# Token sums on VectorE alone and a last down-projection segment of four chunks

## The chip, the cores and the metric

The kernel runs on one core of a Trainium2 chip. The core has TensorE (PE, matrix products), VectorE (DVE), ScalarE (ACT), GpSimd (POOL), SyncE (SP, which here issues the transfers) and DMA engines between DRAM and SBUF. Each engine works through its own list of instructions in order; semaphores join the lists. The metric is the time of one launch in device microseconds. Matmuls write to PSUM banks of 128 x 512 f32, and a bank must be read out before a later group of matmuls may use it again.

## The reference

One layer of an encoder for 256 + 1024 = 1280 tokens with width 1024, all in float32. The change touches the second feed-forward layer and what follows:

```
def swiglu(h, w_gu, w_down):
    gate, up = jnp.split(h @ w_gu, 2, axis=-1)
    return (jax.nn.silu(gate) * up) @ w_down

x = x + 0.5 * rms_norm(swiglu(rms_norm(x, ffn2_pre_g), ffn2_w_gu, ffn2_w_down), ffn2_post_g)
x = rms_norm(x, final_g)
```

The hidden width is 2816, that is 22 chunks of 128. Each f32 product is made of three matmuls of rounded parts (high by high, high by low, low by high), so every operand is split into a high part (a cast on ScalarE) and a low part (a subtraction on VectorE).

## The kernel before

**Order.** The program is written as Python loops, and a scheduler that simulates a timeline sets the order of each engine's list from them and from the dependences. An edit in one place can therefore move instructions of all engines near it.

**Up-projection (`ffn_gu`).** The tokens form three tiles: 0 and 1 with 512 tokens, 2 with 256. The transposed activations of tile t lie in `hT[t]` as parts h and l. Chunks 0 and 1 are "plain": for each tile and each of gate and up (s = 0, 1), `gu` runs 8 x 3 matmuls into a bank `psgu`; then ScalarE takes the silu of the gate, VectorE multiplies it with up (`ac`, L513), and the product is stored to the DRAM tensor `ad`. The tiles run in the order 2, 0, 1 for chunk 0 and 1, 0, 2 for chunk 1. After each half, `post` converts weights and makes pieces of side work.

The other 20 chunks go by `pair`, which computes gate and up of a chunk with seven products where eight would be plain (a scheme of Strassen's kind on 2 x 2 blocks of weights and tokens). For it `token_sums` prepares, once, sums and differences of the token blocks of tiles 0 and 1: T1 to T4, each split in h and l, made in two halves (i = 0, 1) by the steps t1, t3, t2, t4 and by `then`, which overwrites `hT[1]` with T1. Of these sums VectorE does some (`v`), GpSimd four per half (`g`: L459, L471, L472, L478). A VectorE or GpSimd sum is 128 x 1024. Before, the steps begin in chunk 1, two in each `post`.

**Down-projection (`ffn_down`).** The 22 chunks are added up in segments of 1, 3, 3, 3, 3, 3, 3, 3 chunks. In a segment all ten blocks of 128 tokens (b = 0 to 9) run one after another; a block's product of a segment's chunks goes into a pair of banks `psd` (two pairs are in use), and is then copied (segment 0: L660 on VectorE for odd blocks, L662 on ScalarE for even ones) or added (L664, VectorE) to the block's row of y, which lies in the memory of `hT` (tiles named yh0h, yh0l, yh2h). A chunk of weights is loaded as 512 KB `raw` (L612) and split into `wd` (L634 on ScalarE, L635 on VectorE); activations are read back from `ad` as `ar` (L617) and split into `ahl`. `load_to` and `conv_to` walk a list of such units; units ahead of segment 0 are made during the last pair, which `pre` does.

**The end.** In the last segment each finished block goes through `chain`: s1 loads the residual row `xr` (L246) and takes sums of squares (ScalarE L206, then GpSimd's two one-column operations L207 and L208), s2 scales (L212, VectorE) and adds the residual (L254, on GpSimd for blocks 0, 1, 2, 4 and 6, on VectorE for the others), s3 takes the second sum of squares, s4 scales again and sends the row out (L271).

Of the kernel before, what the change touches and what calls it, by code (L numbers as in the profile page):

```python
# [10 lines left out]
F32 = mybir.dt.float32  # L11
# [137 lines left out]
class Trunk:  # L149
# [53 lines left out]
    def rstd(self, src, junk, mul):  # L203
        nc = self.nc
        st = self.stp.tile([P, 2], F32, name="st", tag="st", bufs=8)
        nc.scalar.activation(junk, src, AF.Square, scale=D ** -0.5 / mul, accum_out=st[:, 0:1])  # L206
        nc.gpsimd.tensor_scalar(st[:, 0:1], st[:, 0:1], 1e-6 / (mul * mul), None, op0=OP.add)  # L207
        nc.gpsimd.tensor_tensor(st[:, 1:2], st[:, 0:1], self.mhalf, op=OP.pow)  # L208
        return st[:, 1:2]
# [24 lines left out]
    def chain(self, src, xrows, mul, gpost, gnext, spill=None, out=None, inplace=True):  # L234
# [14 lines left out]
        def s2(b):  # L249
            x, tmp, r = V[b]  # L250
            y = src(b) if inplace else tmp
            self.scaled(y, src(b), r, gpost)
            if inplace:
                (nc.gpsimd if out is None or b in (0, 1, 2, 4, 6) else nc.vector).tensor_tensor(y, y, x, op=OP.add)  # L254
            else:
                nc.gpsimd.tensor_tensor(x, x, y, op=OP.add)
                y = x
            V[b] = y
# [181 lines left out]
    def token_sums(self, tpool):  # L440
        nc = self.nc
        v, g = nc.vector.tensor_tensor, nc.gpsimd.tensor_tensor
        T = {k: [tpool.tile([P, 4, 512], F32R, name=f"T{k}{s}") for s in "hl"] for k in (2, 3, 4)}
# [3 lines left out]
        def split(k, r, src):  # L447
            hi, lo = (z[:, r] for z in T[k])
            nc.scalar.activation(hi, src, AF.Copy)
            v(lo, src, hi.bitcast(F32), op=OP.subtract)  # L450

        for i in range(2):
            r, r2 = slice(2 * i, 2 * i + 2), slice(2 * i + 4, 2 * i + 6)
            b11, b21, b12, b22 = ([z[:, q].bitcast(F32) for z in self.hT[t]] for t in (0, 1) for q in (r, r2))
            Z = {}

            def t1(Z=Z, b11=b11, b12=b12):
                Z[1], Z[0] = self.tmp("x", (P, 2, 512)), self.tmp("g", (P, 2, 512))
                g(Z[0], b12[1], b11[1], op=OP.subtract)  # L459
                v(Z[1], b12[0], b11[0], op=OP.subtract)  # L460
                v(Z[1], Z[1], Z[0], op=OP.add)

            def t2(Z=Z, b22=b22, r=r):
                Z[2] = self.tmp("tmp", (P, 2, 512))
                v(Z[2], b22[0], Z[1], op=OP.subtract)
                v(Z[2], Z[2], b22[1], op=OP.add)
                split(2, r, Z[2])

            def t3(Z=Z, b22=b22, b12=b12, r=r):
                z, o = self.tmp("g", (P, 2, 512)), Z.pop(0)  # L470
                g(o, b22[1], b12[1], op=OP.subtract)  # L471
                g(z, b22[0], b12[0], op=OP.subtract)  # L472
                v(z, z, o, op=OP.add)
                split(3, r, z)

            def t4(Z=Z, b21=b21, r=r):
                z = Z[2]
                g(z, b21[0], z, op=OP.subtract)  # L478
                v(z, z, b21[1], op=OP.add)
                split(4, r, z)  # L480

            first += [t1, t3, t2, t4]
            then.append(lambda Z=Z, r=r: split(1, r, Z[1]))
        return T, first, then

    def ffn_gu(self, pool, tpool, S, W, ad, orders, prep=None):
# [76 lines left out]

        T, first, then = {}, [], []
        for f, order in enumerate(orders):
            for z, t in enumerate(order):
                last = f == len(orders) - 1

                def post(s):
                    n = 2 * f + 3 + (z > 0)  # L570
                    if n <= len(S.units):
                        S.conv_to(n)
                    elif z or s:
                        W.to(1 if first else 3)
                    if last and first:
                        for _ in range(2):
                            first.pop(0)()
                    elif last and then and 1 in order[:z + 1 if s else z]:
                        then.pop(0)()
                gu(f, t, post)  # L580
                if f == 0 and z == 2:
                    t_, a_, b_ = self.token_sums(tpool)
                    T |= t_
                    first += a_
                    then += b_
        for z in first + then:
# [7 lines left out]
    def ffn_down(self, ad, w_down, segs):  # L594
# [26 lines left out]
        def conv_to(n, ahead=3):  # L621
            while st["c"] < min(n, len(units)):
# [13 lines left out]
                st["c"] += 1  # L636
                load_to(min(st["c"] + ahead, npre if st["c"] <= npre and ahead < 3 else 1 << 30))

        pre = [lambda i=i: conv_to(i + 1, 1) for i in range(npre)]

# [538 lines left out]
def run(self):  # L1179
# [124 lines left out]

    def place(c, what):
        if what == "x":
            return pools["p"].tile([P, D], F32, name="xr", tag="wd", bufs=6)
        p = pools.get("p")
        if what == "raw":
            return (p or self.wp).tile([P, D], F32, name="raw", tag="rw" if p else "raw", bufs=2)  # L1310
        if p is None:
# [4 lines left out]
    self.place = place  # L1316
    pre, go = self.ffn_down(ad, a["ffn2_w_down"], (1, 3, 3, 3, 3, 3, 3, 3))
    self.ffn_gu(fa, ft, S2, Pairs(self, a["ffn2_w_gu"], 2, pre), ad, ((2, 0, 1), (1, 0, 2)))
# [48 lines left out]
```

## Time and profile before

The time is the median of 3 runs, 2462.53 us (2461.67 to 2463.34). The profiled execution took 2464.15 us, of which 2462.4 are the span from the first to the last instruction that is shown.

| stage of the profiled execution | us from the span's start |
|---|---|
| plain chunks 0 and 1 of the second layer, token sums beside them | about 1559 to 1622.4 |
| 20 pairs | 1622.4 to about 2120 |
| down-projection, segment 0, overlapping the last pair's end | about 2120 to 2143.1 |
| segments 1 to 7, ten blocks of 4.2 us each | 2143.1 to 2438.2 |
| from the last matmul to the end | 2438.2 to 2462.4 |

How to read it: "busy" is the time in which an engine executes; a wait names the engine, line and tile that the waiting engine was released by. In rows in order of time the first number is the start, the second the duration, and brackets give the idle time before and its releaser. `out<-in` are tiles. Matmuls overlap, so the distance between starts tells their pace, not the duration. The clock is that granted to TensorE, as a share of full speed.

### The profile page before, as it was taken

What the parts mean: (1) busy time and instruction counts of PE and PEld (TensorE: products, weight loads), DVE (VectorE), ACT (ScalarE), POOL (GpSimd) and SP (SyncE); (2) the same over time, 40 slices, a digit from 0 to 9 for tenths busy, and PEclk for the clock granted to TensorE, in tenths of its full rate; (3) what the DMA queues carried; (4) which work ended last, traced back from release to release, by engine and by line L of the source; (5) the groups of instructions that cost most, each with busy time, mean ns of one, the idle gap of its engine ahead of it and who ended that gap; (6) DMA issues with size and microseconds to landing.
All of it is one profiled execution on the core that took longest, in us unless ns stands there. A gap on an engine that the chain in (4) does not pass through costs nothing.

```text
span 2462.4 us, 30177 instructions
## 1 busy us (share of the span) xinstructions
PE 2368.3 (96%) x12028; PEld 2011.2 (82%) x12028; DVE 1270.2 (52%) x1684; ACT 740.0 (30%) x1387; POOL 532.4 (22%) x487
## 2 busy tenths in 40 slices
PE   7999999999999999999988889999999999999995
PEld 7888888888888877888877778888888888788884
DVE  5344444444444448898355553754434434545447
ACT  5211111111111124664365642232222222312113
POOL 2000000000000025796112323532323223000006
PEclk9999999999999999999988899999999999999998
DMA  5111111111111124331276542212222122423224
GB/s 177 43 35 43 35 43 35 43 35 43 35 43 35 43 92 139 92 108 52 86 173 129 127 147 86 75 60 67 73 63 74 59 79 78 141 80 98 76 77 146
DMA packets 191827, 194.92 MB, mean 79 GB/s; under 512 B 30212, under 2 KB 154916, under 8 KB 191686
## 3 DMA queue, kind: packets, MB, share of 16 engines
q1 hardware_dynamic: 191686, 193.00, 26.4%
q8 instruction: 94, 1.54, 0.3%
q14 instruction: 47, 0.39, 0.1%
HBM read 149.23 MB, written 43.73 MB: 78 GB/s over the span
## 4 chain that ended last, share of the span: by engine, by line
PE 85%; DMA 4%; DVE 4%; POOL 2%; ACT 2%; issue 2%; SPq 1%; POOLq 0%; DVEq 0%; ACTq 0%
PE psgu L198 8%; PE psgu L199 8%; PE psgu L200 8%; PE psd L198 8%; PE psd L199 7%; PE psd L200 7%; PE psAB L198 4%; PE psAB L199 4%; PE psAB L200 4%; PE psR L199 2%; PE psR L198 2%; PE psR L200 2%; PE psC L198 2%; PE psC L199 2%; PE psC L200 1%
## 5 line engine op out<-in xcount | busy, mean ns | idle before, releaser
L390 DVE TENSOR_TENSOR y<-y,psd 128x1024 f32<-128x1024 f32 x190 | 231.6, 1219 | 176.2 <-PE psd L200 176.2
L207 POOL TENSOR_SCALAR st<-st 128x1 f32<-128x1 f32 x70 | 38.3, 547 | 1253.5 <-ACT tmp L206 960.7
L371 DVE TENSOR_TENSOR sg<-sg,psgu 128x512 f32<-128x512 f32 (+1 forms) x66 | 39.5, 599 | 272.9 <-PE psgu L200 272.9
L198 PE MATMUL psd<-wd,ahl 128*128 128x512 f32 x440 | 174.6, 397 | 2.5 <-ACT yh0l L662 1.2
L199 PE MATMUL psd<-wd,ahl 128*128 128x512 f32 x440 | 173.9, 395 | 0.0
L200 PE MATMUL psd<-wd,ahl 128*128 128x512 f32 x440 | 173.9, 395 | 0.0
L198 PE MATMUL psd<-whi,ah 128*128 128x512 f32 x432 | 169.7, 393 | 0.8 <-DVE y L407 0.8
L199 PE MATMUL psd<-wlo,ah 128*128 128x512 f32 x432 | 169.3, 392 | 0.0
L90 ACT ACTIVATE whi<-raw 128x1024 fp32r<-128x1024 f32 x98 | 103.3, 1060 | 214.8 <-PE psgu L199 167.2
L200 PE MATMUL psd<-whi,al 128*128 128x512 f32 x432 | 167.7, 389 | 0.0
L198 PE MATMUL psgu<-hT0h,whi 128*128 128x512 f32 (+1 forms) x416 | 156.1, 375 | 0.0
L198 PE MATMUL psgu<-hT1h,whi 128*128 128x512 f32 (+1 forms) x416 | 155.3, 373 | 0.6 <-ACT hT1h L225 0.6
L199 PE MATMUL psgu<-hT0l,whi 128*128 128x512 f32 (+1 forms) x416 | 155.8, 375 | 0.0
L200 PE MATMUL psgu<-hT0h,wlo 128*128 128x512 f32 (+1 forms) x416 | 155.7, 374 | 0.0
L91 DVE TENSOR_TENSOR wlo<-raw,whi 128x1024 fp32r<-128x1024 f32 x98 | 126.7, 1296 | 56.2 <-ACT whi L90 52.8
L199 PE MATMUL psgu<-hT1l,whi 128*128 128x512 f32 (+1 forms) x416 | 155.0, 373 | 0.0
L200 PE MATMUL psgu<-hT1h,wlo 128*128 128x512 f32 (+1 forms) x416 | 155.0, 373 | 0.0
L115 DVE TENSOR_TENSOR wb<-raw,wb 128x512 fp32r<-128x512 f32 x120 | 85.6, 714 | 105.0 <-ACT wb L114 102.6
L114 ACT ACTIVATE wb<-raw 128x512 fp32r<-128x512 f32 x120 | 75.5, 630 | 166.1 <-PE psAB L200 72.9
L741 DVE SCALAR_TENSOR_TENSOR acc<-glu,cv,acc 128x1024 f32<-128x1024 f32 x96 | 121.6, 1285 | 1.8
L198 PE MATMUL psgu<-hT2h,whi 128*128 128x256 f32 x384 | 109.8, 286 | 6.7 <-DVE ac L513 3.6
L372 ACT ACTIVATE ah<-sg 128x512 fp32r<-128x512 f32 (+1 forms) x65 | 35.9, 553 | 252.7 <-DVE sg L371 252.6
(359 smaller groups left out, 6185.7 us busy)
## 6 DMA issues: line engine op xcount, KB each, us to landing
raw<-in_ffn_w_gu_dram SPq DMA_DIRECT2D x88, 512.0 KB
raw<-in_ffn_w_down_dram SPq DMA_DIRECT2D x44, 512.0 KB
ad<-ac SPq DMA_DIRECT2D x44, 256.0 KB
ar<-ad SPq DMA_DIRECT2D x44, 256.0 KB
raw<-in_w_in_dram SPq DMA_DIRECT2D x20, 512.0 KB
x2d<-y SPq DMA_DIRECT2D x10, 512.0 KB
q<-qd SPq DMA_DIRECT2D x16, 320.0 KB
kH<-kd SPq DMA_DIRECT2D x16, 320.0 KB
```

Of the source, the lines that this page charges most:

```text
L90: nc.scalar.activation(hi, raw, AF.Copy)
L91: nc.vector.tensor_tensor(lo, raw, hi.bitcast(F32), op=OP.subtract)
L114: nc.scalar.activation(out[:, 0], src, AF.Copy)
L115: nc.vector.tensor_tensor(out[:, 1], src, out[:, 0].bitcast(F32), op=OP.subtract)
L198: mm(out, lh[0], rh[0], start=first, stop=False, skip_group_check=more)
L199: mm(out, lh[0], rh[1], start=False, stop=False, skip_group_check=more)
L200: mm(out, lh[1], rh[0], start=False, stop=last, skip_group_check=more)
L207: nc.gpsimd.tensor_scalar(st[:, 0:1], st[:, 0:1], 1e-6 / (mul * mul), None, op0=OP.add)
L371: nc.vector.tensor_tensor(s[:, :n], s[:, :n], ps[1][:, :n], op=OP.mult)
L372: nc.scalar.activation(ah, s[:, :n], AF.Copy)
L390: nc.vector.tensor_tensor(yb, yb, o, op=OP.add)
L741: nc.vector.scalar_tensor_tensor(V["acc"], gs(k), w(k), V["acc"], op0=OP.mult, op1=OP.add)
```

## The change

Four things are altered.

1. Token sums: all sums run on VectorE. T3 and T4 are now made from Z1 and Z2 by other differences (T3 from T2's sum, T4 from it in place), so a half has nine sums as three steps of two and one of three. The steps are made from chunk 0's third tile on, one in each `post`.
2. Segments of the down-projection: 1, 3, 3, 3, 3, 3, 2, 4 chunks.
3. Buffers: the raw weight chunks of the down-projection lie in the two temporaries named g, which exist during the pairs already, so two of them are loaded in the last pair (`ahead` is 3 at the last `pre`). The residual rows have a tag of their own with two buffers, in place of the six `wd` buffers. The gains ffn2_post_g and final_g, which share g, are loaded later. `st` has 9 buffers instead of 8.
4. The residual add L254 of the last stage is on VectorE for all ten blocks.

```diff
     def rstd(self, src, junk, mul):
-        st = self.stp.tile([P, 2], F32, name="st", tag="st", bufs=8)
+        st = self.stp.tile([P, 2], F32, name="st", tag="st", bufs=9)
...
-                (nc.gpsimd if out is None or b in (0, 1, 2, 4, 6) else nc.vector).tensor_tensor(y, y, x, op=OP.add)
+                (nc.gpsimd if out is None else nc.vector).tensor_tensor(y, y, x, op=OP.add)
...
+        def t1(i):
+            _, (b11, b21, b12, b22) = blocks(i)
+            z, o = self.tmp("x", (P, 2, 512)), self.tmp("g", (P, 2, 512))
+            Z[1, i] = z
+            v(z, b12[0], b11[0], op=OP.subtract)
+            v(o, b12[1], b11[1], op=OP.subtract)
+            v(z, z, o, op=OP.add)
+
+        def further(i, k, blk, minus):
+            r, b = blocks(i)
+            z = Z[1, i] if k == 2 else Z[2, i]
+            if k == 2:
+                Z[2, i] = o = self.tmp("tmp", (P, 2, 512))
+            else:
+                o = self.tmp("g", (P, 2, 512)) if k == 3 else z
+            if minus:
+                v(o, b[blk][0], z, op=OP.subtract)
+                v(o, o, b[blk][1], op=OP.add)
+            else:
+                v(o, z, b[blk][0], op=OP.subtract)
+                v(o, o, b[blk][1], op=OP.subtract)
+            split(k, r, o)
+
         for i in range(2):
-            def t1(Z=Z, b11=b11, b12=b12):
-                Z[1], Z[0] = self.tmp("x", (P, 2, 512)), self.tmp("g", (P, 2, 512))
-                g(Z[0], b12[1], b11[1], op=OP.subtract)
...
-            first += [t1, t3, t2, t4]
-            then.append(lambda Z=Z, r=r: split(1, r, Z[1]))
+            first += [lambda i=i: t1(i), lambda i=i: further(i, 2, 3, True), lambda i=i: further(i, 3, 0, False),
+                      lambda i=i: further(i, 4, 1, True)]
+            then.append(lambda i=i: split(1, blocks(i)[0], Z[1, i]))
...
+            if t == 1 and not T:
+                t_, a_, b_ = self.token_sums(tpool)
...
+            if first:
+                first.pop(0)()
+            elif then and 1 in gone:
+                then.pop(0)()
...
-                load_to(min(st["c"] + ahead, npre if st["c"] <= npre and ahead < 3 else 1 << 30))
+                load_to(st["c"] + ahead)
 
-        pre = [lambda i=i: conv_to(i + 1, 1) for i in range(npre)]
+        pre = [lambda i=i: conv_to(i + 1, 1 if i < npre - 1 else 3) for i in range(npre)]
...
         if what == "x":
-            return pools["p"].tile([P, D], F32, name="xr", tag="wd", bufs=6)
+            return p.tile([P, D], F32, name="xr", tag="xr", bufs=2)
         if what == "raw":
-            return (p or self.wp).tile([P, D], F32, name="raw", tag="rw" if p else "raw", bufs=2)
+            return self.tmp("g")
...
-    pre, go = self.ffn_down(ad, a["ffn2_w_down"], (1, 3, 3, 3, 3, 3, 3, 3))
+    pre, go = self.ffn_down(ad, a["ffn2_w_down"], (1, 3, 3, 3, 3, 3, 2, 4))
```

TensorE's list keeps its order. What moves on the others is shown at three places; line numbers behind the edits are larger by 2 or 3 in the changed kernel (L513 becomes L515, L634 L637, L635 L638, L660 L663, L662 L665, L664 L667, L612 L615).

VectorE beside the plain chunks, before: from the product `ac` of chunk 0's last tile to that of chunk 1's first (L459 to L479 are the sums, L450 the low parts, L226 transposes of the last tile).

```order
L513 TENSOR_TENSOR ac<-ac,psgu 128x512
L450 TENSOR_TENSOR T4l<-tmp,T4h 128x1024
L450 TENSOR_TENSOR T2l<-tmp,T2h 128x1024
L473 TENSOR_TENSOR g<-g 128x1024
L450 TENSOR_TENSOR T3l<-g,T3h 128x1024
L479 TENSOR_TENSOR tmp<-tmp,hT0l 128x1024
L450 TENSOR_TENSOR hT1l<-x,hT1h 128x1024
L115 TENSOR_TENSOR wb<-g,wb 128x512
L450 TENSOR_TENSOR hT1l<-x,hT1h 128x1024
L450 TENSOR_TENSOR T4l<-tmp,T4h 128x1024
L513 TENSOR_TENSOR ac<-ac,psgu 128x512
```

The same piece now:

```order
L515 TENSOR_TENSOR ac<-ac,psgu 128x512
L476 TENSOR_TENSOR tmp<-tmp,hT0l 128x1024
L476 TENSOR_TENSOR tmp<-tmp,hT1l 128x1024
L450 TENSOR_TENSOR T4l<-tmp,T4h 128x1024
L478 TENSOR_TENSOR g<-tmp,hT0h 128x1024
L450 TENSOR_TENSOR T2l<-tmp,T2h 128x1024
L450 TENSOR_TENSOR hT1l<-x,hT1h 128x1024
L479 TENSOR_TENSOR g<-g,hT0l 128x1024
L115 TENSOR_TENSOR wb<-g,wb 128x512
L475 TENSOR_TENSOR tmp<-hT0h,tmp 128x1024
L450 TENSOR_TENSOR hT1l<-x,hT1h 128x1024
L515 TENSOR_TENSOR ac<-ac,psgu 128x512
```

The second half's sums for T4 stand ahead of the product, and its last low part has moved behind it.

ScalarE in segment 0, before: copies of even blocks (L662), conversions of activations (ahl) and weights (wd) for the next segment.

```order
L662 ACTIVATE yh0h<-psd 128x1024
L634 ACTIVATE ahl<-ar 128x512
L662 ACTIVATE yh0h<-psd 128x1024
L634 ACTIVATE ahl<-ar 128x512
L662 ACTIVATE yh0l<-psd 128x1024
L634 ACTIVATE wd<-raw 128x1024 x2
L662 ACTIVATE yh0l<-psd 128x1024
L634 ACTIVATE ahl<-ar 128x512
L662 ACTIVATE yh2h<-psd 128x1024
```

and now:

```order
L665 ACTIVATE yh0h<-psd 128x1024
L637 ACTIVATE ahl<-ar 128x512
L665 ACTIVATE yh0h<-psd 128x1024
L637 ACTIVATE wd<-g 128x1024 x2
L637 ACTIVATE ahl<-ar 128x512
L665 ACTIVATE yh0l<-psd 128x1024 x2
L637 ACTIVATE wd<-g 128x1024 x2
L637 ACTIVATE ahl<-ar 128x512
L665 ACTIVATE yh2h<-psd 128x1024
```

Two weight conversions stand ahead of the copy of block 4, where they stood ahead of that of block 6, and two more ahead of that of block 8. SyncE's list, which had two weight loads behind the last store to `ad`, has two residual loads there, with the weight loads behind them.

VectorE at the end of the last segment, before (yh0l are blocks 4 to 7, yh2h blocks 8 and 9):

```order
L664 TENSOR_TENSOR yh2h<-yh2h,psd 128x1024
L212 SCALAR_TENSOR_TENSOR yh0l<-yh0l,st,g 128x1024 x2
L254 TENSOR_TENSOR yh0l<-yh0l,xr 128x1024
L212 SCALAR_TENSOR_TENSOR yh2h<-yh2h,st,g 128x1024
L254 TENSOR_TENSOR yh2h<-yh2h,xr 128x1024
L212 SCALAR_TENSOR_TENSOR yh0l<-yh0l,st,g 128x1024
L212 SCALAR_TENSOR_TENSOR yh2h<-yh2h,st,g 128x1024 x2
L254 TENSOR_TENSOR yh2h<-yh2h,xr 128x1024
L212 SCALAR_TENSOR_TENSOR yh2h<-yh2h,st,g 128x1024
```

and now:

```order
L667 TENSOR_TENSOR yh2h<-yh2h,psd 128x1024
L254 TENSOR_TENSOR yh2h<-yh2h,xr 128x1024
L212 SCALAR_TENSOR_TENSOR yh0l<-yh0l,st,g 128x1024
L212 SCALAR_TENSOR_TENSOR yh2h<-yh2h,st,g 128x1024 x2
L254 TENSOR_TENSOR yh2h<-yh2h,xr 128x1024
L212 SCALAR_TENSOR_TENSOR yh2h<-yh2h,st,g 128x1024
```

Behind the last block's addition, two scalings of yh0l, block 7's residual and one scaling of yh2h are gone: they stand ahead of it.

More of the change, by code (lines that the diff above doesn't have):

```diff
@@ L441, in token_sums @@
         nc = self.nc
-        v, g = nc.vector.tensor_tensor, nc.gpsimd.tensor_tensor
+        v = nc.vector.tensor_tensor
         T = {k: [tpool.tile([P, 4, 512], F32R, name=f"T{k}{s}") for s in "hl"] for k in (2, 3, 4)}
@@ L450, in split @@
             v(lo, src, hi.bitcast(F32), op=OP.subtract)
-        for i in range(2):
-            r, r2 = slice(2 * i, 2 * i + 2), slice(2 * i + 4, 2 * i + 6)
-            b11, b21, b12, b22 = ([z[:, q].bitcast(F32) for z in self.hT[t]] for t in (0, 1) for q in (r, r2))
-            Z = {}
-            def t1(Z=Z, b11=b11, b12=b12):
-                Z[1], Z[0] = self.tmp("x", (P, 2, 512)), self.tmp("g", (P, 2, 512))
-                g(Z[0], b12[1], b11[1], op=OP.subtract)
[L460 to L480, printed above, removed]
-            first += [t1, t3, t2, t4]
-            then.append(lambda Z=Z, r=r: split(1, r, Z[1]))
@@ new lines, in token_sums, with blocks @@
+        Z = {}
+        def blocks(i):
+            r, r2 = slice(2 * i, 2 * i + 2), slice(2 * i + 4, 2 * i + 6)
+            return r, [[z[:, q].bitcast(F32) for z in self.hT[t]] for t in (0, 1) for q in (r, r2)]
+        def t1(i):
[5 more added lines that the diff above has]
+            v(z, z, o, op=OP.add)
@@ L562, in pair, with post @@
                     store(f, 2, a2)
-        T, first, then = {}, [], []
+        T, first, then, gone = {}, [], [], set()
+        def post(f, t, z, s):
+            n = 2 * f + 3 + (z > 0)
+            if n <= len(S.units):
+                S.conv_to(n)
+            elif z or s:
+                W.to(1 if first else 3)
+            if t == 1 and not T:
+                t_, a_, b_ = self.token_sums(tpool)
+                T.update(t_)
+                first.extend(a_)
+                then.extend(b_)
+            if first:
+                first.pop(0)()
+            elif then and 1 in gone:
+                then.pop(0)()
         for f, order in enumerate(orders):
             for z, t in enumerate(order):
[L567 to L585, printed above, removed]
+                gu(f, t, lambda s: post(f, t, z, s))
+                if f:
+                    gone.add(t)
         for z in first + then:
@@ L1305, in place @@
     def place(c, what):
+        p = pools.get("p")
         if what == "x":
-            return pools["p"].tile([P, D], F32, name="xr", tag="wd", bufs=6)
-        p = pools.get("p")
+            return p.tile([P, D], F32, name="xr", tag="xr", bufs=2)
         if what == "raw":
-            return (p or self.wp).tile([P, D], F32, name="raw", tag="rw" if p else "raw", bufs=2)
+            return self.tmp("g")
         if p is None:
```

## The prediction

> **What bounds the kernel now.** I read the page's busy line first, then the waits of TensorE over the second feed-forward layer and the tail, then windows that cut the program into stages, and last the time-ordered rows of the few places that these name. The page:
>
> ```profile
> PE 2368.3 (96%) x12028; PEld 2011.2 (82%) x12028; DVE 1270.2 (52%) x1684; ACT 740.0 (30%) x1387; POOL 532.4 (22%) x487
> ```
>
> TensorE is busy 96% of the span. Its instructions keep their number and order, so only 94 us could go anywhere. TensorE's waits from 1500 us on (us in total, times, longest):
>
> ```profile
> PE psgu L198 <- DVE ac L513: 3.6, 1, 3.6
> PE psgu L198 <- DVE hT1l L226: 3.1, 1, 3.1
> PE psd L198 <- ACT yh0l L662: 1.2, 1, 1.2
> PE psd L198 <- DVE yh0l L664: 0.8, 1, 0.8
> PE psd L198 <- DVE yh0h L660: 0.5, 1, 0.5
> PE psAB L198 <- DVE tmp L549: 0.3, 1, 0.3
> ```
>
> The windows (from and to, length, busy PE, PEld, DVE, ACT and POOL with their instructions, clock, DMA share, GB/s):
>
> ```profile
> 1619.20:1622.40 3.20, 3.20 (x17) 3.20 (x17) 1.96 (x4) 1.42 (x5) 1.67 (x1) 0.51 0.34 125
> 1622.40:2120.00 497.60, 497.60 (x2615) 425.63 (x2614) 202.64 (x297) 137.57 (x238) 137.22 (x95) 1.00 0.23 71
> 2438.20:2462.40 24.20, 0.20 (x1) 0.00 (x0) 16.32 (x12) 6.68 (x12) 12.78 (x14) 0.58 0.36 138
> ```
>
> The pair stage (1622 to 2120) is full of matmuls and has nothing to give. Four places have: the stall on ac L513, the first down-projection segment with its stalls on L660 and L662, the stall on L664 near the end, and 24.2 us behind the last matmul. The stall on L226 lies ahead of the first edit and stays. The sum is made against the profiled execution's 2464.15 us (its span 2462.4 and 1.75 around it), 1.6 above the median of 2462.53.
>
> **Token sums.** VectorE in order of time (start, duration):
>
> ```profile
> 1573.41 4.56 DVE L460 TENSOR_TENSOR x<-hT1h,hT0h 128x1024 f32<-128x1024 f32 x2
> ...
> 1604.41 1.21 DVE L450 TENSOR_TENSOR T2l<-tmp,T2h 128x1024 fp32r<-128x1024 f32 x1
> 1605.55 1.21 DVE L473 TENSOR_TENSOR g<-g 128x1024 f32<-128x1024 f32 x1
> 1607.89 2.23 DVE L450 TENSOR_TENSOR T3l<-g,T3h 128x1024 fp32r<-128x1024 f32 x1 [1.13 <-ACT T3h L449]
> ...
> 1617.35 0.67 DVE L513 TENSOR_TENSOR ac<-ac,psgu 128x512 f32<-128x512 f32 x1
> ```
>
> One of GpSimd's sums, and then TensorE around its stall:
>
> ```profile
> 1597.16 3.38 POOL L471 TENSOR_TENSOR g<-hT1l 128x1024 f32<-128x1024 f32 x1
> ```
>
> ```profile
> 1614.17 0.28 PE L200 MATMUL psgu<-hT2h,wlo 128*128 128x256 f32 x1
> 1618.08 0.39 PE L198 MATMUL psgu<-hT2h,whi 128*128 128x256 f32 x1 [3.63 <-DVE ac L513]
> ...
> 1622.43 0.51 PE L198 MATMUL psAB<-hT0h,wb 128*128 128x512 f32 x1
> ```
>
> A 128x1024 sum on VectorE costs 1.14 from start to start where GpSimd idles (1604.41 to 1605.55), and 2.2 to 2.3 each while GpSimd's, 3.4 long, run (1573.41, 1607.89). Eight of those go. In the new order, from 1573.41 up to the product that ends at 1618.02 now, VectorE has 23 sums and splits at 1.14 and four half-size operations at 0.6: 28.6 us, to 1602.0. Five splits stand ahead of it that may wait for ScalarE's rounding, by 1.13 each as at 1607.89: 1607.7. TensorE asks for the bank at 1614.3, so 6.6 us of cover remain, and the stall goes. Behind it the clock stood at 0.51 for 3.2 us. Matmuls issued 0.12 apart up to 1614.17 then took 0.21. Without either, the 24 matmuls of this half end at 1614.29 + 24 x 0.12 = 1617.2, and the pair stage starts there instead of at 1622.43: **-5.2**. If the slow clock comes anyway, only the wait goes, -3.6. The earlier start adds steps behind the first chunk's third tile; the rows of that stretch are the ones just counted. Weights of the pair stage are split on GpSimd too, which is freer by 8 x 3.4 = 27 us.
>
> **Into the down-projection.** The chain of waits shows what holds the first segment now:
>
> ```profile
> 2130.24 2.90 DMA ad<-ac
> ...
> 2133.59 4.59 DMA raw<-in_ffn_w_down_dram
> 2138.18 0.02 issue
> 2138.20 0.86 ACT wd L634
> 2139.06 0.11 issue
> 2139.17 1.01 ACT yh0l L662
> ```
>
> The last product's store lands at 2133.1, only then are two weight chunks loaded (4.6 us), and ScalarE converts them ahead of a block's copy L662 that TensorE needs. After the change two raw chunks come during the last pair, and this load is gone from the chain. The converted chunks still lie in memory of the pool that replaces the product tiles, so conversion waits for the same landing at 2133.1. Two conversions of about 1.0 (2138.20 to 2139.17) then stand ahead of the copy of block 4, on ScalarE, and on VectorE two splits of 1.2 (rows below) with an ahl split of 0.7 ahead of that of block 5. The copy of block 4 runs 2135.8 to 2136.8, which makes TensorE wait about 0.95. The third weight load can only be issued when VectorE has freed a raw buffer (about 2135.5). With some 3.7 us of landing (one chunk, where two at once took 4.59), ScalarE's 1.0 and VectorE's 1.2 it is queued ahead of the copy of block 7, so block 9 starts at 2142.85 and segment 1 at 2144.3 instead of 2143.1: **+1.2**. From below: the 1.2 wait on L662 goes without a new one, less some 0.4 by that third load, -0.8. From above: the two residual loads that now stand behind the last store slow store and weights, and the third chunk comes 1.8 later, +3.
>
> Segment 6 has two chunks, so a block is 2 x 1.4 = 2.8 us (six matmuls of 0.233 a chunk), and four chunks, eight activation slices and two gains have to come in 28 us. VectorE's rows of two such splits and the addition behind them, at a change of segment now:
>
> ```profile
> 2311.14 1.22 DVE L635 TENSOR_TENSOR wd<-raw,wd 128x1024 fp32r<-128x1024 f32 x1
> 2312.28 1.22 DVE L664 TENSOR_TENSOR yh2h<-yh2h,psd 128x1024 f32<-128x1024 f32 x1
> ```
>
> Two weight splits of 1.2 ahead of an addition delay it by about 2.4. With two bank pairs and blocks of 2.8 the addition may be late by a block less its own 1.2; counted so over the new order, the tightest place (last block of segment 5, first of segment 6) keeps 0.4 to 1.0. I take **0**, and +2 as the upper bound for one load that comes late.
>
> **The end.** Two groups of the rows from 2398 us on (count, busy, mean ns, idle before and its releaser):
>
> ```profile
> L208 POOL TENSOR_TENSOR st<-st,mhalf 128x1 f32<-128x1 f32 x20 | 17.0, 852 | 1.4
> L212 DVE SCALAR_TENSOR_TENSOR yh0h<-yh0h,st,g 128x1024 f32<-128x1024 f32 x8 | 12.1, 1513 | 7.1 <-POOL st L208 7.1
> ```
>
> One of GpSimd's residuals, and VectorE to the end:
>
> ```profile
> 2437.73 2.35 POOL L254 TENSOR_TENSOR yh0l<-yh0l,xr 128x1024 f32<-128x1024 f32 x1
> ```
>
> ```profile
> 2437.89 3.28 DVE L212 SCALAR_TENSOR_TENSOR yh0l<-yh0l,st,g 128x1024 f32<-128x1024 f32 x1
> 2441.09 1.21 DVE L664 TENSOR_TENSOR yh2h<-yh2h,psd 128x1024 f32<-128x1024 f32 x1
> ...
> 2454.05 1.22 DVE L254 TENSOR_TENSOR yh2h<-yh2h,xr 128x1024 f32<-128x1024 f32 x1
> 2457.51 1.28 DVE L212 SCALAR_TENSOR_TENSOR yh2h<-yh2h,st,g 128x1024 f32<-128x1024 f32 x1 [2.24 <-POOL st L208]
> ```
>
> At 2437.9 a residual on GpSimd and a scaling on VectorE overlap, and the scaling takes 3.28 instead of 1.28. The last block's addition starts only at 2441.09, 2.9 after the last matmul, and the chain of earlier blocks is still in the queue. After the change a block costs VectorE 1.21 + 2 x 1.28 + 1.22 = 5.0 us against TensorE's 4 x 1.4 = 5.6, so VectorE keeps up; the stall on L664 goes, **-0.8**. Behind the last matmul then stand, in the new order: last addition (1.2), residual of block 8 (1.2), its second square and root (2.2: 2455.27, where the residual ends now, to 2457.51), the last block's first scaling beside it, the scaling of block 8 (1.2), the last residual (1.2), square and root (2.2), last scaling to end of span (2457.51 to 2462.4, 4.9): 14.2. For GpSimd's one-column operations that VectorE holds up (L208's mean is 852 ns) I add 0.5: 14.7 against 24.2, **-9.5**. Below: the last block's own chain alone, 1.2 + 2.2 + 1.2 + 1.2 + 2.2 + 4.9 + 0.3 of semaphores = 13.2, so -11.0. Above: each of two roots held twice by 1.2, less the 0.5 counted: 14.7 + 1.9 + 0.6 for the output = 17.2, so -7.0.
>
> The Trainium skill (SBUF — State Buffer, section "Who interferes with whom") has it that a VectorE instruction with two SBUF inputs contends with a GpSimd instruction that reads SBUF. The trace agrees (3.28 against 1.28 above), and the rule speaks against putting all residuals on VectorE, as they now hold off the one-column roots: by it the tail would be nearer its upper bound, 17.2 us, and the sum 2.5 smaller.
>
> **Sum:** -5.2 + 1.2 + 0 - 0.8 - 9.5 = -14.3. On the median: 2462.5 - 14.3 = **2448.2 us**. All lower bounds together: -5.2 - 0.8 - 0.8 - 11.0 = -17.8, 2444.7. All upper ones: -3.6 + 3 + 2 - 0.8 - 7.0 = -6.4, 2456.1.
>
> **Rivals.**
> *Roots set the tail.* With no residuals on it, GpSimd has only one-column work, but VectorE is busy 5.0 of 5.6 us with two-input operations, and L208 takes 852 ns on the mean where an operation on one column could be far shorter. Then the tail is 17 to 18.5: 2451 to 2452. Against it: behind the last matmul VectorE has idle time. Chance 0.10.
> *Loads late.* The weights of segment 1 or of segment 7 come late, as each has only two raw buffers and the transfer takes longer than a short block: +3 to +5, so 2451 to 2453. For it: the 4.59 us transfer above. Against it: 12 loads in segment 6 are 3.8 MB in 28 us, 137 GB/s, and the tail of now moves 138. Chance 0.10.
> *The sums' gain is lost.* If weights of the first pair, or VectorE with the sums it took over, hold TensorE just as long, the first term is nothing: 2453.4. Against it: 6.6 us of cover. Chance 0.05. Any two of these three together come to about 2456 to 2459: chance 0.07.
> *Slower: the last segment falls behind VectorE's queue.* In its order the scalings wait for roots, and the additions that free TensorE's banks stand behind them. 5.0 us of work and 1.0 of waiting at each of two scalings make 7.0 per block; ten blocks of 7.0 instead of 5.6 take 14 us, all that is gained, so this is the point from which it decides. At 1.6 per wait a block is 8.2: 2448.2 + 26 = 2474. For it: L212 waited 7.1 us over eight instructions, 0.9 each. Against it: some of that is time in which nothing else was to be done, and roots waited behind the 2.4 us residuals that go. Chance 0.04.
>
> **How the numbers follow.** Forecast 0.64, the rivals in their order 0.10, 0.10, 0.05, 0.07 (two together) and 0.04. This kernel's times can be told apart by about 0.2%, 4.9 us, so faster means below 2457.6. The forecast and the first three rivals lie there (0.89), and a little of two together (0.02): 0.91. No change gets the rest of those, 0.05, slower 0.04. The range is that of the bounds: 2444.7 to 2456.
>
> **What would show it.** The wait on the product behind the sums is gone, the first psAB matmul comes near 1617 and the clock there is 1.00; GpSimd has no 128x1024 sums before it. The pair stage keeps 497.6 us. Segment 1 starts some 24.3 us after the pair stage's last full block (2120 now) with a wait on a block's copy by ScalarE of about 1. The two-chunk segment takes 28 us, the four-chunk one 56 without waits. From the last matmul to the end 14 to 15 us. It is wrong if the four-chunk segment takes over 60 us, if the tail stays above 18, or if the pair stage starts later than 1619.

## The result, and the profile after

The changed kernel takes 2441.76 us (median of 6 runs, 2438.86 to 2444.29) against 2463.30 for the kernel before (6 runs, 2461.67 to 2464.63): a ratio of 0.9913, 95% interval 0.990 to 0.9926. A second set of runs gave 2441.03. So it gains 21.5 us where 14.3 were forecast, and ends 3 us below the range. The profiled execution is the quickest of its six, 2438.86 us with a span of 2437.1; the kernel before's was 2464.15 with 2462.4. Between these two 25.3 us have to be found.

The busy times of the changed kernel:

```profile
PE 2350.7 (96%) x12028; PEld 2009.4 (82%) x12028; DVE 1263.2 (52%) x1695; ACT 739.9 (30%) x1387; POOL 491.5 (20%) x474
```

TensorE has the same 12028 instructions, in the same order but for the grouping of chunks in the last two segments, and is busy 17.6 us less. That can't come from a removed wait. TensorE's waits from 1500 us on:

```profile
PE psgu L198 <- DVE hT1l L226: 2.8, 1, 2.8
PE psd L198 <- DVE yh0l L663: 1.4, 1, 1.4
PE psd L198 <- ACT yh0l L665: 0.7, 1, 0.7
PE psd L198 <- DVE yh0l L667: 0.6, 1, 0.6
PE psd L198 <- DVE yh0h L663: 0.5, 1, 0.5
PE psAB L198 <- DVE tmp L551: 0.3, 1, 0.3
```

The wait on the product `ac` is gone. The copies in segment 0 (L663, L665) now make TensorE wait 2.6 us in all instead of 1.7. Windows of the changed kernel, columns as before:

```profile
1556.50:1559.50 3.00, 3.00 (x16) 3.00 (x16) 2.70 (x3) 1.54 (x3) 1.52 (x3) 0.50 0.48 143
1614.90:2107.10 492.20, 492.20 (x2619) 425.85 (x2618) 201.39 (x295) 136.98 (x237) 137.00 (x95) 1.00 0.23 72
2417.90:2437.10 19.20, 0.09 (x1) 0.00 (x0) 11.04 (x10) 4.82 (x10) 7.27 (x10) 0.55 0.37 137
```

The pair stage, which the prediction took to have "nothing to give", is 492.2 us long instead of 497.6, at the same clock of 1.00. And the stretch behind the last matmul is 19.2 us instead of 24.2, not 14.7. By stage, from marks on TensorE that both traces have (start of the second layer's up-projection, first psAB, last psR, last matmul, end of span):

| stage | before | changed | difference | forecast |
|---|---|---|---|---|
| up to the second layer's first psgu | 1559.0 | 1555.3 | -3.7 | 0 |
| plain chunks and token sums | 63.4 | 59.7 | -3.8 | -5.2 |
| pairs | 497.9 | 492.0 | -5.9 | 0 |
| down-projection | 317.6 | 310.6 | -7.0 | +0.4 |
| behind the last matmul's start | 24.4 | 19.5 | -4.9 | -9.5 |

The first row lies ahead of the work that was reordered and differs from run to run: a second profile of the changed kernel has 1558.4 there. The two stages that should have changed most changed less than forecast, and 12.9 us came in two that should have stayed nearly as they were. Two windows of equal length in the down-projection, where nearly all matmuls have 512 columns, show how. Before:

```profile
2210.00:2250.00 40.00, 40.00 (x173) 32.25 (x172) 20.78 (x22) 7.89 (x12) 0.00 (x0) 1.00 0.29 89
```

Changed:

```profile
2210.00:2250.00 40.00, 40.00 (x179) 33.10 (x178) 19.98 (x23) 8.00 (x12) 0.00 (x0) 1.00 0.29 89
```

With TensorE busy throughout and the same granted clock, 40 us hold 173 matmuls before and 179 now. From start to start over 2150 to 2400 us that is 233.3 and 226.7 ns (means of 1071 and 1102 intervals). Both paces were in the kernel before too: its first layer's up-projection goes at 226.7.

### The profile page after: what moved, and what is told of

Same layout as the page of the kernel before. It is cut to its first block, busy times and chain, and to the rows that moved or that the text cites. A ratio compares the mean times of both kernels' runs of the same rounds, so it can differ in the third digit from the quotient of the medians.

```text
span 2437.1 us, 30173 instructions
## 1 busy us (share of the span) xinstructions
PE 2350.7 (96%) x12028; PEld 2009.4 (82%) x12028; DVE 1263.2 (52%) x1695; ACT 739.9 (30%) x1387; POOL 491.5 (20%) x474
## 4 chain that ended last, share of the span: by engine, by line
PE 87%; DMA 5%; DVE 3%; ACT 2%; issue 1%; POOL 1%; SPq 1%; POOLq 0%; ACTq 0%; DVEq 0%
PE psgu L198 9%; PE psgu L199 9%; PE psgu L200 9%; PE psd L198 7%; PE psd L199 7%; PE psd L200 7%; PE psAB L198 4%; PE psAB L199 4%; PE psAB L200 4%; PE psR L199 2%; PE psR L200 2%; PE psR L198 2%; PE psC L198 2%; PE psC L199 2%; PE psC L200 1%; PE psqk L198 1%
## 5 line engine op out<-in xcount | busy, mean ns | idle before, releaser
L207 POOL TENSOR_SCALAR st<-st 128x1 f32<-128x1 f32 x70 | 41.7, 596 | 1253.4 <-ACT tmp L206 981.8
L198 PE MATMUL psd<-wd,ahl 128*128 128x512 f32 x440 | 172.1, 391 | 3.3 <-DVE yh0l L663 1.4
L199 PE MATMUL psd<-wd,ahl 128*128 128x512 f32 x440 | 171.3, 389 | 0.0
L200 PE MATMUL psd<-wd,ahl 128*128 128x512 f32 x440 | 171.2, 389 | 0.0
```

Source lines behind the costliest of these rows:

```text
L198: mm(out, lh[0], rh[0], start=first, stop=False, skip_group_check=more)
L199: mm(out, lh[0], rh[1], start=False, stop=False, skip_group_check=more)
L200: mm(out, lh[1], rh[0], start=False, stop=last, skip_group_check=more)
```

## The experiments

**What two theories say of the pace.** STATE: TensorE leaves the 3.6 us stall on `ac` and the slow clock behind it in a slower mode and keeps it; the new token sums remove the stall and with it the mode. ADDRESS: the pace goes by where a matmul's operands start in SBUF. For this the compiled programs give the start addresses (bytes in a partition, one buffer of each tile):

```
tile                          before    changed
T2h (pairs, moving)           129216    129248
T4h (pairs, moving)           161984    162016
wd  (down-proj., moving)      133312    133344
hT0h (up-proj., moving)        17632     17632
wb  (pairs, stationary)       204768    204768
ahl (down-proj., stationary)  212960    212960
```

"Moving" is the operand of 512 columns that streams through, "stationary" the loaded one. Tiles that are allocated behind `st` on its side of SBUF lie 32 bytes further on, because `st` has 9 buffers (of 8 bytes each) instead of 8. In the kernel before, 2220 matmuls of 512 columns (those of T2 to T4 and of wd, and half of the output projection) have a moving operand at 0 modulo 64 and a stationary one at 32; in the changed kernel all 7920 have both at 32.

**The kernel before, moved by 32 bytes with an unused tile.**

```diff
         self.stp = ctx.enter_context(tc.tile_pool(name="stp", bufs=4))
+        self.stp.tile([P, 8], F32, name="pad", tag="pad", bufs=1)
```

> The kernel before with one 32-byte tile (8 floats per partition, never used) ahead of all later SBUF tiles of its side, so that T2 to T4, the converted down-projection weights wd and half of the output-projection weights start at 32 instead of 0 modulo 64 bytes. Instructions and their order are those of the kernel before. Theory ADDRESS (a 128x512 matmul issues every 233.3 ns when its moving operand starts at 0 modulo 64 and every 226.7 ns at 32): 2220 matmuls x 6.7 ns = 14.8 us less, 2448.5 us, and the first psAB still starts near 1620 behind the 3.6 us stall. Theory STATE (TensorE leaves the stall on the product behind the token sums in a slower mode and keeps it): no change, 2463 us, 233 ns from 1640 on.

Measured: 2449.9 us against 2463.31 beside it, ratio 0.9945 (0.993 to 0.996). The stall on `ac` is still there with 3.6 us, and wd goes at 226.7 ns. STATE falls: no instruction and no wait was changed. The pair stage is 492.4 us, the down-projection 310.7.

**The kernel before with the change's own line.**

```diff
-        st = self.stp.tile([P, 2], F32, name="st", tag="st", bufs=8)
+        st = self.stp.tile([P, 2], F32, name="st", tag="st", bufs=9)
```

> The kernel before with 9 instead of 8 buffers for st, the one line of the change that seemed to do nothing. Order unchanged; all SBUF tiles behind st move by 32 bytes, as with the unused tile. ADDRESS: the same time as with that tile, about 2449.5 us, 226.7 ns per matmul of wd, with the 3.6 us stall on the product still there. STATE, or a use of the ninth buffer itself: no change in pace, 233.3 ns.

Measured: 2448.32 us against 2463.68, ratio 0.9943 (0.9925 to 0.996). Its window, with the 3.6 us wait on `ac` still there:

```profile
2210.00:2250.00 40.00, 40.00 (x178) 33.15 (x177) 19.98 (x22) 8.01 (x12) 0.00 (x0) 1.00 0.27 85
```

So on the kernel before one line that touches no instruction's order gives 13 (the tile) to 15 us (the line).

**The changed kernel, moved back.** The same unused tile in the changed kernel.

> The changed kernel with the same unused 32-byte tile: the tiles it moved to 32 modulo 64 bytes go back to 0 modulo 64 (0 modulo 128, where the kernel before had 64). Order unchanged. ADDRESS: 14.8 us more than the changed kernel, about 2456.5 us, 233 ns per 128x512 matmul of wd. If only 64 modulo 128 is slow: no change from 2441.8. STATE: no change, 226.7 ns, since the stall stays away.

Measured: 2449.87 us (ratio to before 0.9946, 0.993 to 0.9963), 8 to 9 more than the changed kernel's medians. The pace is 233.3 ns, and the two stages in question are 498.0 and 317.8 us, 13.1 longer together. 64 modulo 128 and 0 modulo 128 are both slow. That the median moved by less than the two stages: its profile has no slow clock behind the wait on L226 (plain chunks 58.2 instead of 59.7) and starts the second layer 1.4 earlier; both differ from run to run, and I can't account for the rest.

```profile
2210.00:2250.00 40.00, 40.00 (x173) 32.13 (x172) 19.53 (x21) 7.38 (x11) 0.00 (x0) 1.00 0.27 87
```

**The token sums alone.** The kernel before with `token_sums` and `post` of the change.

> The kernel before with the token sums of the change alone (all on VectorE, one step per post from the first chunk's third tile on); buffers, segments, residuals and tile addresses as before. ADDRESS: the 3.6 us stall and the slow clock behind it go, 3.6 to 5.2 us less, about 2458.5 us, and the matmuls of wd stay at 233 ns. STATE: the stall is gone and with it the slow mode, about 2444 us with 226.7 ns.

Measured: 2458.63 us, ratio 0.9978 (0.9968 to 0.9987), so 4.7 us less. TensorE's waits in that kernel have no `ac` any more, and its pace stays:

```profile
PE psgu L198 <- DVE hT1l L226: 3.0, 1, 3.0
PE psd L198 <- ACT yh0l L665: 0.9, 1, 0.9
PE psd L198 <- DVE yh0l L667: 0.8, 1, 0.8
PE psd L198 <- DVE yh0h L663: 0.4, 1, 0.4
PE psAB L198 <- DVE tmp L551: 0.3, 1, 0.3
```

```profile
2210.00:2250.00 40.00, 40.00 (x173) 32.25 (x172) 20.03 (x22) 7.89 (x12) 0.00 (x0) 1.00 0.28 89
```

This is the prediction's first term, and STATE has fallen a second time: the stall is gone, the slow pace is not.

**Which addresses are fast.** Four more placements of the changed kernel, by unused tiles at one or both ends of SBUF. First the stationary operands (and what else lies at that end) moved to 0 modulo 64:

```diff
+        self.rp = ctx.enter_context(tc.tile_pool(name="rp", bufs=1, side="right"))
+        self.rp.tile([P, 8], F32, name="pad")
```

> The changed kernel with an unused 32-byte tile at the other end of SBUF, so that the tiles allocated from there (weights of the up-projections, wb, ahl and others) move to 0 modulo 64; the order is unchanged. Of the 128x512 matmuls 1860 then have a moving operand at 0 modulo 64 (most of them the first feed-forward layer's down-projection, whi and wlo), and 5820 have the moving one at 32 and the stationary one at 0. ADDRESS, by the moving operand alone: 1860 x 6.7 ns = 12.4 us more, about 2454 us; the down-projection of the first layer (35 to 949 us) goes at 233 ns, that of the second stays at 226.7. ADDRESS, by a difference between moving and stationary operand: the second layer's matmuls of wd (32 and 0) go to 233 ns, the first layer's (0 and 0) stay at 226.7, about 42 us more, 2484 us. STATE: no change.

Measured: 2468.23 us, 26.5 more. The matmuls of wd (moving 32, stationary 0) go at 233.3 ns, so it is not the moving operand alone. But the total is below the 42 us of a plain rule of likeness, and in the first layer's down-projection (0 and 0) the means were 228 to 231, neither of the two values. A part of the gap is that matmuls of 256 columns behave the other way: beside the same move they go at 116.8 ns from start to start instead of 119.6. Then both at 0 modulo 64 (the same tile, and one of 32 bytes in the pool of constants):

> The changed kernel with an unused 32-byte tile at both ends of SBUF, so that the moving and the stationary operand of every 128x512 matmul start at 0 modulo 64 bytes (in the changed kernel both start at 32). Order unchanged. Theory RELATION (fast when moving and stationary operand start alike modulo 64): no change from the changed kernel, 2441.8 us, 226.7 ns per matmul of wd. Theory ZERO (slow whenever one of the two starts at 0): all 7920 go at 233.3 ns, about 40 us more, 2480 us or above.

Measured: 2446.6 us (ratio to before 0.9933, 0.9918 to 0.9948), 5 more than the changed kernel; wd at 228.9 ns. Neither theory: 0 and 0 modulo 64 is a third of the way from fast to slow. Then 64 bytes at one end, and 32 and 96 at the two ends:

> The changed kernel with an unused 64-byte tile ahead of nearly all tiles of one side of SBUF. The moving and the stationary operand of the matmuls of wd and of the pairs then both start at 32 modulo 64 bytes, but at 32 and 96 modulo 128. Order unchanged. If start addresses modulo 64 decide: 226.7 ns per matmul of wd and no change, 2441.5 us. If they must be alike modulo 128: 233 ns (or the 228.9 ns of 0 and 64 modulo 128), 13 to 35 us more.

> The changed kernel with unused tiles at both ends of SBUF so that moving and stationary operand of every 128x512 matmul start at 0 modulo 128 bytes (the run with both at 0 modulo 64 had 0 and 64 modulo 128 for wd and gave 228.9 ns). Order unchanged. If operands need only start alike modulo 128: 226.7 ns, 2441.5 us. If 0 modulo 64 costs something by itself: 228.9 ns, about 2447 us.

Measured: 2455.54 us with 232.5 ns, and 2473.53 us with 232.3 ns. The first came out as expected if starts must be alike modulo 128, but the second, where they are, fits neither of its expectations. The windows of these four kernels in the order told:

```profile
2210.00:2250.00 40.00, 40.00 (x173) 32.11 (x172) 20.79 (x22) 8.00 (x12) 0.00 (x0) 1.00 0.29 89
```

```profile
2210.00:2250.00 40.00, 40.00 (x176) 32.79 (x176) 20.35 (x22) 7.90 (x12) 0.00 (x0) 1.00 0.29 89
```

```profile
2210.00:2250.00 40.00, 40.00 (x173) 32.41 (x172) 20.17 (x22) 7.89 (x12) 0.00 (x0) 1.00 0.29 89
```

```profile
2210.00:2250.00 40.00, 40.00 (x174) 32.44 (x173) 20.28 (x22) 8.01 (x12) 0.00 (x0) 1.00 0.26 77
```

All placements that were tried, for the matmuls of wd (mean from start to start, 2150 to 2400 us):

| moving, modulo 128 | stationary, modulo 128 | moving less stationary, modulo 256 | ns | kernel |
|---|---|---|---|---|
| 96 | 96 | 0 | 226.7 | changed; before with 9 buffers |
| 0 | 64 | 64 | 228.9 | both at 0 modulo 64 |
| 0 | 0 | 128 | 232.3 | both at 0 modulo 128 |
| 32 | 96 | 64 | 232.5 | 64 bytes at one end |
| 96 | 64 | 32 | 233.3 | stationary moved |
| 64 | 96 | 224 | 233.3 | before |
| 0 | 96 | 32 | 233.3 | changed, moved back |

One placement of seven gives the fast pace, and it is the one in which most of the kernel before already stood. The third column, from the same compiled programs, shows what the tests modulo 64 and 128 missed: that placement is the only one with both starts equal modulo 256, and "both at 0 modulo 128" has them 128 apart. No kernel was made to test this, but the output projection (the last 95 us ahead of the second layer's up-projection) holds both cases side by side. In six of the kernels (before, moved back, and the four placements) its weights lie at two places, and in each the matmuls with equal starts modulo 256 (at 0, 32 or 224) have a mean of 227.2 to 228.3 ns and the others, between them in time, of 233.1 to 233.4.

Two things show that this is not the whole rule. The 232.5 of the fourth row is the mean of two paces: 233.3 up to 2354.8 us and 228.9 from there on, the second block of the two-chunk segment, with no wait of TensorE and no change of the starts modulo 256:

```profile
2310.00:2350.00 40.00, 40.00 (x173) 32.42 (x172) 18.63 (x21) 5.50 (x10) 0.00 (x0) 1.00 0.30 89
2360.00:2400.00 40.00, 40.00 (x176) 32.81 (x176) 23.01 (x23) 7.75 (x14) 3.40 (x6) 1.00 0.21 66
```

And in the same kernel the first layer's down-projection keeps the equal starts that it has in the changed kernel (224), but goes at 230.5 ns on the mean instead of 228.1, mostly in blocks of 6 or 12 matmuls between others whose starts now lie 64 apart. So what ran before seems to count too; why is open. Shown is that moving tiles alone, with the order of instructions kept, changes the pace between 226.7 and 233.3 ns.

**The end: residuals.** In the changed kernel with GpSimd's residuals put back:

```diff
-                (nc.gpsimd if out is None else nc.vector).tensor_tensor(y, y, x, op=OP.add)
+                (nc.gpsimd if out is None or b in (0, 1, 2, 4, 6) else nc.vector).tensor_tensor(y, y, x, op=OP.add)
```

> The changed kernel with the residual of blocks 0, 1, 2, 4 and 6 back on GpSimd; addresses as in the changed kernel. Theory RING (in the last segment a block's add, square, root, scaling, residual, second square, root and scaling follow each other through VectorE's list in order, so waits for roots set the pace): the residual of 2.4 us on GpSimd lengthens the ring and delays roots, the stretch behind the last matmul grows from 19.4 to 21 to 23 us, 2444 to 2446 us. Theory LOAD (VectorE is simply full): VectorE loses 6 us of work, the stretch falls to about 17 us, 2439.5 us.

Measured: 2441.5 us, as the changed kernel's 2441.0 and 2441.8. Neither theory by the median. In its profile the stretch behind the last matmul is the same 19.4 us, but a wait of 2.6 on an addition (L667) appears ahead of it, with a clock of 0.50 for 2.8 us behind it, and the down-projection is 315.0 us instead of 310.6. By the stages the residuals on VectorE are worth some 4 us, by medians nothing; these runs don't settle it.

**The end: segments.** The changed kernel with three chunks in each of the last two:

```diff
-    pre, go = self.ffn_down(ad, a["ffn2_w_down"], (1, 3, 3, 3, 3, 3, 2, 4))
+    pre, go = self.ffn_down(ad, a["ffn2_w_down"], (1, 3, 3, 3, 3, 3, 3, 3))
```

> The changed kernel with segments of 1, 3, 3, 3, 3, 3, 3, 3 chunks. In the last segment a block is then 4.1 us of TensorE instead of 5.4. If VectorE's pace there (4.95 us of work and 1.55 of waits for roots a block, 6.5 us) sets the end in both, the ten blocks end as late after the segment's start as now: the last segment starts 13.6 us later and the end comes 8 to 13 us later than in the changed kernel, 2450 to 2455 us. If the longer last segment gave nothing: no change, 2441.8 us.

Measured: 2442.69 us (ratio 0.9917, 0.9902 to 0.9932), about 1 us more, where 8 to 13 were expected. The profile has 22.0 us behind the last matmul's start instead of 19.5, and the same 310.6 before it. VectorE's pace in the changed kernel is not its own limit: with shorter blocks the additions and scalings of neighbouring blocks fill each other's waits (the three groups of L212 wait 7.6 us for L208 there, 15.5 in the changed kernel). So the long last segment brings 1 (medians) to 2.5 us (this stage).

**The end: roots.** Groups of the changed kernel from 2365 us on:

```profile
L207 POOL TENSOR_SCALAR st<-st 128x1 f32<-128x1 f32 x20 | 16.0, 800 | 288.9 <-ACT x L206 259.9 <-ACT tmp L206 28.8
...
L208 POOL TENSOR_TENSOR st<-st,mhalf 128x1 f32<-128x1 f32 x20 | 12.2, 610 | 1.7
L212 DVE SCALAR_TENSOR_TENSOR yh0h<-yh0h,st,g 128x1024 f32<-128x1024 f32 x8 | 10.3, 1282 | 5.6 <-POOL st L208 5.6
L212 DVE SCALAR_TENSOR_TENSOR yh0l<-yh0l,st,g 128x1024 f32<-128x1024 f32 x8 | 10.3, 1282 | 5.3 <-POOL st L208 5.3
...
L212 DVE SCALAR_TENSOR_TENSOR yh2h<-yh2h,st,g 128x1024 f32<-128x1024 f32 x4 | 5.1, 1284 | 4.6 <-POOL st L208 4.6
```

An addition of one column takes 0.80 us on the mean. VectorE waits 15.5 us for 20 roots: 3.8 behind its last addition, 11.7 between the first and the last. There a block costs it 5.9 us (nine steps from 2368.18 to 2421.17), more than TensorE's 24 x 0.227 = 5.4. (The 6.5 of the expectation above spreads all 15.5 over ten blocks.) The last block in order of time, VectorE and then GpSimd:

```profile
2421.17 1.21 DVE L667 TENSOR_TENSOR yh2h<-yh2h,psd 128x1024 f32<-128x1024 f32 x1
2422.30 1.22 DVE L254 TENSOR_TENSOR yh2h<-yh2h,xr 128x1024 f32<-128x1024 f32 x1
2423.43 1.28 DVE L212 SCALAR_TENSOR_TENSOR yh0l<-yh0l,st,g 128x1024 f32<-128x1024 f32 x1
2425.48 1.28 DVE L212 SCALAR_TENSOR_TENSOR yh2h<-yh2h,st,g 128x1024 f32<-128x1024 f32 x1 [0.77 <-POOL st L208]
2427.53 1.28 DVE L212 SCALAR_TENSOR_TENSOR yh2h<-yh2h,st,g 128x1024 f32<-128x1024 f32 x1 [0.77 <-POOL st L208]
```

```profile
2423.73 1.06 POOL L207 TENSOR_SCALAR st<-st 128x1 f32<-128x1 f32 x1 [1.75 <-ACT tmp L206]
2424.88 0.57 POOL L208 TENSOR_TENSOR st<-st,mhalf 128x1 f32<-128x1 f32 x1
2425.53 1.31 POOL L207 TENSOR_SCALAR st<-st 128x1 f32<-128x1 f32 x1
```

The last block's addition begins 3.3 us after the last matmul (2417.60 and 0.23 more), and L207 ends (2424.79, 2426.84) when a scaling on VectorE ends (2424.71, 2426.76). To take that operation off GpSimd in the last segment alone (there `chain` calls `rstd` with `act` set):

```diff
-        nc.gpsimd.tensor_scalar(st[:, 0:1], st[:, 0:1], 1e-6 / (mul * mul), None, op0=OP.add)
+        if act:
+            nc.scalar.activation(st[:, 0:1], st[:, 0:1], AF.Copy, bias=1e-6 / (mul * mul))
+        else:
+            nc.gpsimd.tensor_scalar(st[:, 0:1], st[:, 0:1], 1e-6 / (mul * mul), None, op0=OP.add)
```

> The changed kernel with the addition of epsilon (L207, one column) in the last segment on ScalarE instead of GpSimd; GpSimd keeps the power L208. L207 takes 0.80 us on the mean in the changed kernel, 0.22 at its shortest. RING with L207 held back by VectorE: each root is shorter by about 0.6 us, waits for roots fall from 0.78 to 0.3 us, VectorE needs 5.5 us a block and keeps up with TensorE; behind the last matmul 15 to 16.5 us, 2438 to 2439 us. Rival: the hold-up only moves to L208, which then is first on GpSimd behind ScalarE: no change, 2441.8 us.

Measured: 2435.12 us, ratio to before 0.9888 (0.9874 to 0.9903), 6 us less than the changed kernel. Groups of this kernel, L211 and L215 being the power and the scaling:

```profile
L211 POOL TENSOR_TENSOR st<-st,mhalf 128x1 f32<-128x1 f32 x20 | 17.4, 873 | 297.1 <-ACT st L208 296.9
L215 DVE SCALAR_TENSOR_TENSOR yh0l<-yh0l,st,g 128x1024 f32<-128x1024 f32 x8 | 10.2, 1282 | 2.1 <-POOL st L211 2.1
L215 DVE SCALAR_TENSOR_TENSOR yh0h<-yh0h,st,g 128x1024 f32<-128x1024 f32 x8 | 10.2, 1282 | 5.7 <-POOL st L211 5.6
L215 DVE SCALAR_TENSOR_TENSOR yh2h<-yh2h,st,g 128x1024 f32<-128x1024 f32 x4 | 5.1, 1283 | 3.0 <-POOL st L211 3.0
```

The hold-up does move to the power (0.61 to 0.87 us), as the rival had it, but only part of it: waits fall from 15.5 to 10.7 us, the stretch behind the last matmul's start from 19.5 to 16.4, and the last addition begins 1.0 after the last matmul. This stage and the down-projection (309.5 instead of 310.6) account for 4.2 of the 6 us; where the rest lies is not shown.

**A version that beats both.** The same operation on ScalarE in all five norms, beside one more measurement of the changed kernel.

> The changed kernel with the addition of epsilon on ScalarE in all five norms, not in the last segment alone (that gave 2435.1 us). Roots held back elsewhere: each shorter root that TensorE waits for (transposes behind scalings: 9.2, 3.8 and 2.1 us of waits on L212) saves some tenths, 2431 to 2434 us. If ScalarE's extra 0.2 us delays other work as much: 2435 us.

> The changed kernel once more, beside the next two. If pace goes by addresses: 226.7 ns per matmul of wd again, 310.6 us from the last full pair's psR to the last matmul, 19.4 us behind it, total 2439 to 2444 us. If the pace of its first profile was chance: 233 ns in this one.

Measured: 2432.94 us (ratio to before 0.9883, 0.9864 to 0.9901) and 2441.03. The first is the quickest kernel here; that it is better than the one before it by 2 us lies within the spread of their runs (2432.3 to 2436.6 and 2433.5 to 2436.7). The repeated kernel has 226.7 ns, 310.6 and 19.5 us again: in these two profiles the stages repeat to 0.1, where medians of the whole can't tell 2 us. Two profiles don't show that they always do: the 4 us of the residuals above appear in a stage and in no median.

## Why the prediction was right or wrong

**Wrong: "nothing to give".** The prediction said that TensorE's instructions keep their number and order and concluded that the pair stage keeps its 497.6 us. It named the ninth `st` buffer nowhere. That line moved the operands of 2220 matmuls and made each 6.7 ns shorter: 14.8 us by that count, 13 to 15 measured on the kernel before. The trace of before showed it, had it been asked: 233.3 ns for one loop and 226.7 for another of the same shape at the same clock of 1.00. I took 0.233 for the cost of a matmul, and 512 columns for all there was to know of it.

**Right in mechanism: token sums.** The stall on `ac` went, with no other wait in its place, -5.2 forecast, -4.7 measured alone. In the pair of profiles it shows as -3.8, since the changed kernel's execution had a clock of 0.50 for 3 us behind the wait on L226 and the other had 1.00 there:

```profile
1560.20:1563.20 3.00, 3.00 (x28) 3.00 (x27) 2.70 (x3) 1.78 (x3) 1.52 (x3) 1.00 0.43 126
```

**Right: the transition.** Forecast +1.2: from the last psR to the first matmul of segment 1 (the 61st of the down-projection) it took 22.8 us before and takes 23.9, +1.1. The copy of block 4 waits for conversions behind the last store, 0.66 where 0.95 was forecast, and block 9 waits 1.45 for the copy of block 7 that stands behind the third weight chunk's split. ScalarE's rows of the changed kernel:

```profile
2119.70 2.01 ACT L637 ACTIVATE wd<-g 128x1024 fp32r<-128x1024 f32 x2 [1.22 <-DMA ad<-ac]
2121.61 0.62 ACT L637 ACTIVATE ahl<-ar 128x512 fp32r<-128x512 f32 x1
2122.13 1.00 ACT L665 ACTIVATE yh0l<-psd 128x1024 f32<-128x1024 f32 x1
```

**Right: the two-chunk segment.** No wait of TensorE falls into it; it takes 27.3 us where 28 were forecast.

**Mis-sized: the end.** -9.5 forecast, -4.9 measured, outside the term's bounds (-7.0 to -11.0); the tail of 19.2 us is above the 18 that the prediction named as a sign of being wrong. The step that failed is "VectorE keeps up", from 5.0 us of work against 5.6 of TensorE. Work alone was counted. With waits for roots it is 5.9 against 5.4, and the last addition starts 3.3 us late, where the sum took nothing and the kernel before had 2.9. What was gained lies behind it: 15.9 us from the last addition's start to the end, 21.3 before, 14.7 forecast. There two of the three roots take 0.8 and 1.1 us longer than the third (L207 with 1.06 and 1.31 against 0.22), where 0.5 was added in all. That is the rival "roots set the tail", which forecast 17 to 18.5 us and so was still short; additions behind scalings that wait for roots are the slower rival's mechanism too, whose break-even at 7.0 us a block was not reached. The sentence on the shared access of VectorE and GpSimd (the Trainium skill, SBUF — State Buffer, "Who interferes with whom"), set aside in the sum, gave 17.2: nearer than the 14.7 of the sum, and L207 ending with VectorE's instructions agrees with it.

**The sum.** -4.7 (sums), -13 to -15 (placement), -4.9 (the end), +1.1 (transition) and -0.2 (the wait on L664, 0.8 before and 0.6 now) make -22 to -24, against -21.5 measured; the terms come from different runs. Without the placement the change would stand at 2449.9 (the changed kernel moved back) to 2455 (this sum without it), where 2448.2 was forecast: the two misses lay on opposite sides, and the one that no term covered was the larger.

## What to carry to other kernels

Where the same shape of matmul goes at two paces under one clock, compare start addresses of both operands before anything else, modulo 256 too, and read every edit to a buffer count as a move of all that is allocated behind it. An engine keeps up with another only if its waits inside the loop are counted with its work: take the ring of dependent steps, not the sum of busy times. And put one-column operations where no long instruction of another engine holds them.

## What the hardware showed that was not expected

A 128x512 f32 matmul takes 226.7 to 233.3 ns by the placement of its operands, with the granted clock at 1.00 throughout; with both starts equal modulo 256 it was 226.7 to 228.3 on the mean, but for the first layer's down-projection named above. One of 256 columns takes 119.6 ns with equal starts (the changed kernel) and 116.8 with starts 32 apart (the stationary moved), so the best place for one shape isn't that for the other. A move of 32 bytes was worth 15 us of 2463, and the worst placement tried made the changed kernel 32 us slower (2473.5 against 2441.5). The Trainium skill (TensorE: Matmul & The Clock Gate, section "Step-by-step: what each phase is for") states that TensorE reads the streaming and the loaded operand through two independent ports and that loading the next weights takes no read bandwidth from the running matmul. The table of placements does not sit well with that as a statement on time: with the moving operand at 96, the place of the stationary one alone made 226.7 or 233.3 ns. Whether the two meet in SBUF is not shown.

The half clock behind a wait of about 3 us comes or not in executions with nearly the same wait: behind 2.8 us in the changed kernel it was 0.50 for 3 us, and behind the 3.1 us in the kernel before the 256-column matmuls went on at 0.12 us. The Trainium skill (the same page, section "What's actually happening") has the clock watch an activity window that runs free of the program and vary from run to run; the traces agree.
